# RMS norm and matrix product on one core: sixteen early words of output, smaller loads and last stores, and a last store issued outside the ordered section

## Chip, cores and metric

The kernel runs on one core of a Trainium2 chip. The metric is the device time of one execution in microseconds (us); the median of several executions counts, and less is better. The profile comes from one further look at a single execution with the hardware profiler on.

## What is computed

Each row of x (16 x 1024 rows of 512 numbers, float32) is divided by the root of its mean square, multiplied by gamma, and multiplied by a weight matrix of 512 x 768. The output is float32, 16 x 1024 x 768.

```
rms = np.sqrt(np.mean(x ** 2, axis=-1, keepdims=True) + eps)
x_norm = x / rms * gamma
return np.matmul(x_norm, weight).astype(np.float32)
```

So 33.6 MB of x and 1.6 MB of weights come in, and 50.3 MB of output go out.

## The kernel before

**Tiles.** The 16,384 rows are 128 tiles of 128 rows (NT). x is loaded in groups of 16 tiles (XG) into two buffers, xt0 and xt1; in a group each of the 128 partitions holds 16 rows that follow each other in memory. The output is collected in groups of 8 tiles (OG) in three buffers, ot0 to ot2, and stored from there. What one load or one store covers is set at lines 136 and 137 by `stretches`: a dictionary that gives, for some groups, the sizes into which the group is cut; a group without an entry is one transfer. In x, group 0 is cut into 2, 2, 4 and 8 tiles, groups 1, 2, 5, 6 and 7 into 8 and 8, and groups 3 and 4 (tiles 48 to 79) are whole. In the output, group 0 is cut into 2, 2 and 4, group 1 and the last one into 4 and 4, and all others are whole. A store of 8 tiles is 3 MB, a load of 16 tiles 4 MB.

**Work on a tile.** ScalarE squares the rows and sums them (`square`, L194), and takes the root of several tiles' sums at once (`root`, L199); VectorE inverts it (L201). GpSimd turns x into bf16 (`cast`, L186, and `cast_quad`, L258). Then x has to be transposed: for most tiles TensorE does it (L228) and VectorE copies the result out of PSUM (`evac`, L237); for the last four tiles of each later group VectorE transposes blocks of 32 x 32 (`move`, L269). The products run on TensorE: for each of four blocks of 128 features the transposed x is held (L294) and two products with the weights follow (L298), 512 and 256 wide. The finished tile is scaled on its way from PSUM to the output buffer by ScalarE (even tiles, L277) or VectorE (odd tiles, L279). The weights have been multiplied by gamma at the start by the same two lines.

**Order.** Nothing is issued while the program is described. `run` and `transfer` append each operation with the cells that it reads and writes to a list in the class `Order`. At the end `emit` walks through the list once. It keeps, for each engine, what that engine already knows to be done (`known`, a clock for each other engine and for each transfer), and finds the few waits that are needed (`needs`). Then it goes through the list again, puts the waits on the engines and issues the operations in the order of the list; each engine's queue holds its own in that order. A transfer gets a semaphore from a small set that is used again once some engine's knowledge shows that the earlier transfer on it has landed.

All of this stands in a critical section (L432). `emit` returns the marks of those transfers that no operation waited for, and a second section makes the SyncE queue (SP) wait for them (L435):

```
    with tc.tile_critical():
        left = order.emit()

    with tc.tile_critical():
        for sem, count in left:
            SP.wait_ge(sem, count)
```

**Queues.** All loads of x (L175), both weight loads (L343) and all stores (L291) are issued by SP, in one queue, in the order of the list: the first two tiles of x, the two weight loads, the rest of the first two x groups, and from there on stores as their tiles are finished, with the loads of a later x group between them. A store waits on SP for the last tile of its stretch; whatever is behind it on SP waits too. gamma alone is loaded by ScalarE's queue (L338). L468 is the line that the profile gives for what frames the kernel: branches, waits and the closing barrier of all engines.

Of the kernel before, what the change touches and what calls it, by code (L numbers as in the profile page):

```python
# [11 lines left out]
F32 = mybir.dt.float32  # L12
# [4 lines left out]
P = 128  # L17
# [3 lines left out]
class Order:  # L21
# [17 lines left out]
    def emit(self):  # L39
        nc = self.tc.nc  # L40
        streams = {id(e): n for n, e in enumerate((nc.tensor, nc.vector, nc.scalar, nc.gpsimd, nc.sync))}
        writer, readers = {}, {}
        known = [dict() for _ in streams]
        clocks, needs, place, slot_of, slots = [], [], [], {}, []
        count = [0] * len(streams)
        for n, (proc, engine, _, reads, writes) in enumerate(self.ops):
            at = streams[id(engine)]
            if proc is None:
                me, turn = ("transfer", n), 1
            else:  # L50
                count[at] += 1
                me, turn = at, count[at]
            written = {writer[cell] for cell in reads + writes if cell in writer}
            read = {d for cell in writes for d in readers.get(cell, ())}
            need = []
            for d in sorted(written | read, reverse=True):
                who, when = place[d]
                if who == me and (engine is nc.tensor or d not in written):
                    continue
                if known[at].get(who, 0) < when:  # L60
                    need.append(d)
                    for k, v in clocks[d].items():
                        known[at][k] = max(known[at].get(k, 0), v)
            if proc is None:
                free = [k for k, d in enumerate(slots) if known[at].get(("transfer", d), 0)]
                if free:
                    slots[free[0]] = n
                else:
                    slots.append(n)
                slot_of[n] = ("slot", slots.index(n))  # L70
            clock = dict(known[at])
            clock[me] = turn
            place.append((me, turn))
            clocks.append(clock)
            needs.append(need)
            for cell in reads:
                readers.setdefault(cell, []).append(n)
            for cell in writes:
                writer[cell], readers[cell] = n, []
        awaited = {d for need in needs for d in need}  # L80
        last = [n for n, (me, _) in enumerate(place) if not isinstance(me, int) and n not in awaited]
        sems, marks, done = {}, {}, {}
        for n in range(len(self.ops)):
            me = slot_of.get(n, place[n][0])
            if n in slot_of or n in awaited:
                if me not in sems:
                    sems[me] = self.tc.alloc_semaphore(f"done{len(sems)}")
                done[me] = done.get(me, 0) + (16 if n in slot_of else 1)
                marks[n] = (sems[me], done[me])
        for n, (proc, engine, issue, _, _) in enumerate(self.ops):  # L90
            for d in needs[n]:
                engine.wait_ge(*marks[d])  # L92
            ins = issue()
            if n in marks:
                ins.then_inc(marks[n][0], 16 if n in slot_of else 1)
        return [marks[n] for n in last]


@with_exitstack
def kernel(  # L100
# [8 lines left out]
    nc = tc.nc  # L109
    PE, DVE, ACT, POOL, SP = nc.tensor, nc.vector, nc.scalar, nc.gpsimd, nc.sync  # L110
    order = Order(tc)
# [5 lines left out]
    out = out.flatten_outer_dims()  # L117
    N, D = x.shape
    _, O = out.shape
    K = D // P  # L120
    NT = N // P
    NP = NT // 2
    XG, OG = 16, 8
    AHEAD = 20

    def stretches(group, parts):
        first, size, i = {}, {}, 0
        for g in range(NT // group):
            for n in parts.get(g, [group]):
                for t in range(i, i + n):  # L130
                    first[t], size[t] = i, n
                i += n
        return first, size

    last = NT // OG - 1
    x_first, x_size = stretches(XG, {0: [2, 2, 4, 8], **{g: [8, 8] for g in (1, 2, 5, 6, 7)}})
    o_first, o_size = stretches(OG, {0: [2, 2, 4], 1: [4, 4], last: [4, 4]})

    def rows(ap, i, n):
        base, t = (x_first[i], x_size[i]) if i < XG else (i - i % XG, XG)  # L140
        return ap[base * P:(base + t) * P, :].rearrange("(p t) d -> p t d", t=t)[:, i - base:i - base + n, :]

    def sb(name, shape, dtype):
        return nc.alloc_sbuf_tensor(name, shape, dtype).ap()
# [14 lines left out]
    ot = [sb(f"ot{n}", [P, OG, O], F32) for n in range(3)]  # L159
# [7 lines left out]
    def cells(name, slot, i, n=1):  # L167
        return [(name, slot, t) for t in range(i, i + n)]
# [4 lines left out]
    def load(i):  # L173
        dst, to = x_of(i, x_size[i])
        order.transfer(SP, lambda: SP.dma_start(out=dst, in_=rows(x, i, x_size[i])), writes=to)  # L175
# [3 lines left out]
    def load_until(i):  # L179
        while starts and starts[0] < i:  # L180
            load(starts.pop(0))
# [104 lines left out]
    def store(i):  # L286
        first, n = o_first[i], o_size[i]
        s = first // OG % 3
        if i == first + n - 1:
            src = ot[s][:, first % OG:first % OG + n, :]  # L290
            order.transfer(SP, lambda: SP.dma_start(out=rows(out, first, n), in_=src), reads=cells("ot", s, first % OG, n))  # L291

    def hold(lhsT, cell):
        run(PE, lambda: PE.ldweights(lhsT), [cell])  # L294
# [20 lines left out]
    def finish_tile(i, a, engine):  # L315
        s = i // OG % 3

        before = [("ot", s, i % OG - 1)] if i == o_first[i] + o_size[i] - 1 else []
        scale(engine, ot[s][:, i % OG, :], ops[a][:, :O], rstd[:, i:i + 1],
              [("ops", a, 0), ("ops", a, 1), ("rstd", i)] + before, [("ot", s, i % OG)])  # L320
        store(i)
# [20 lines left out]
    def load_weights(h):  # L342
        order.transfer(SP, lambda: SP.dma_start(out=w_f32[:, 2 * h:2 * h + 2, :].rearrange("p c o -> p (c o)"), in_=wv[:, h, :]),  # L343
                       writes=[("w_f", 2 * h), ("w_f", 2 * h + 1)])

    load_until(2)
    load_weights(0)
    load_weights(1)
    load_until(2 * XG)
# [79 lines left out]
            matmuls(i, a, range(K), feed)  # L429
            finish_tile(i, a, engine)  # L430

    with tc.tile_critical():  # L432
        left = order.emit()

    with tc.tile_critical():  # L435
        for sem, count in left:
            SP.wait_ge(sem, count)


# [33 lines left out]
```

## Time and profile before

| what | value |
|---|---|
| median of 7 executions | 209.79 us (209.57 to 210.37) |
| the profiled execution's own time | 209.57 us |
| its span, first to last instruction | 207.6 us |
| mean granted TensorE clock | 0.985 |
| HBM read, written | 35.13 MB, 50.33 MB |
| stores: 8 tiles, 4 tiles, 2 tiles | 13, 5, 2 |
| loads of x: 16 tiles, 8 tiles, 4, 2 | 2, 11, 1, 2 |

The page gives busy time by engine, then the span in 40 slices of 5.2 us each, then the DMA queues, and then the chain of work that ended last, followed back from the last instruction. "q1" is the queue that SP feeds; its share is the time that its packets took, as a share of sixteen DMA engines over the span. A row of the windows view gives, for one stretch of time, the busy time and number of instructions of each engine, the granted clock, the mean busy share of the sixteen DMA engines, and GB/s; packets are counted where they start, so a short window's share can be above 1. The lines for one source line give the durations of its instructions and, for a transfer, the time from its issue to its landing, which is when the last of its sixteen completion marks has come. In the timeline, what stands in square brackets is the engine's idle time before the instruction and what ended it.

The time of an execution is longer than the span of its instructions; here by 1.9 us.

### The profile page before, as it was taken

How to read it: one execution, taken by the hardware profiler on the slowest of the kernel's cores; microseconds unless marked ns; L12 is line 12 of the kernel's file. 1: busy time of each engine (PE TensorE's matmuls, PEld its weight loads, DVE VectorE, ACT ScalarE, POOL GpSimd, SP SyncE). 2: the span in 40 equal slices, each digit the busy share in tenths (PEclk: the TensorE clock that was granted, in tenths of full speed). 3: DMA queues.
4: the chain of work that ended last, by engine and by line, in shares of the span. 5: the costliest groups of instructions: out<-in, count | busy, mean ns of one | idle time of the engine just before them, and what ended most of it. 6: DMA issues, size and time to landing. Idle time of an engine off the chain costs nothing.

```text
span 207.6 us, 2784 instructions
## 1 busy us (share of the span) xinstructions
PE 194.9 (94%) x1236; PEld 72.7 (35%) x717; DVE 149.4 (72%) x255; ACT 144.4 (70%) x343; POOL 59.9 (29%) x34
## 2 busy tenths in 40 slices
PE   7889999999999999999999999999999999999910
PEld 1234434433344334332344334333343333343300
DVE  0455647998589957998579975999579975999410
ACT  4698897877768596855887687777787687763300
POOL 2247642046300390005800670007600363000000
PEclk9999999999999999999999999999999999999995
DMA  6999999999999999999999999999999999996994
GB/s 228 418 447 423 376 389 430 429 442 420 445 437 436 409 434 450 423 417 425 434 426 426 421 434 429 423 425 431 443 423 428 415 448 434 421 436 260 440 421 199
DMA packets 5488, 85.62 MB, mean 412 GB/s; under 512 B 610, under 2 KB 612, under 8 KB 1380
## 3 DMA queue, kind: packets, MB, share of 16 engines
q1 hardware_dynamic: 5472, 85.46, 97.2%
q8 instruction: 7, 0.11, 0.2%
q14 instruction: 5, 0.04, 0.0%
q10 hardware_dynamic: 4, 0.00, 0.0%
HBM read 35.13 MB, written 50.33 MB: 412 GB/s over the span
## 4 chain that ended last, share of the span: by engine, by line
PE 71%; DMA 16%; DVE 5%; issue 1%; SPq 1%; ACT 1%; POOL 1%; ACTq 0%
PE ps L298 63%; DMA xt<-in_x_dram 16%; PE ps L228 8%; DVE ot L279 2%; DVE xTq L269 2%; DVE xT L237 1%; POOL xb L186 1%; ACT jk L194 0%; SPq L343 0%; SPq L175 0%; ACT ot L277 0%; SPq L291 0%; DVE rstd L201 0%; SPq L468 0%; ACTq L92 0%
## 5 line engine op out<-in xcount | busy, mean ns | idle before, releaser
L298 PE MATMUL ps<-w_bf,xT 128*128 128x512 bf16 (+1 forms) x800 | 147.7, 326 | 0.8 <-ACT ot L277 0.4
L277 ACT ACTIVATE ot<-ps,rstd 128x768 f32<-128x768 f32 x64 | 57.5, 898 | 42.9 <-PE ps L298 41.3
L194 ACT ACTIVATE jk<-xt 128x512 bf16<-128x512 f32 x128 | 78.7, 618 | 6.8 <-DMA xt<-in_x_dram 6.8
L186 POOL CAST xb<-xt 128x2048 bf16<-128x2048 f32 (+3 forms) x21 | 46.4, 2221 | 112.4 <-DMA xt<-in_x_dram 112.4
L279 DVE TENSOR_SCALAR ot<-ps,rstd 128x768 f32<-128x768 f32 x64 | 64.8, 1013 | 9.0 <-PE ps L298 8.4
L294 PEld LDWEIGHTS <-xT 128*128 128x128 bf16 x400 | 39.3, 98 | 59.9 <-issue 52.0
L228 PE MATMUL ps<-ident_f,xb 128*128 128x128 f32 x200 | 54.4, 277 | 0.9 <-POOL xb L186 0.9
L237 DVE COPY xT<-ps 128x1024 bf16<-128x1024 bf16 (+1 forms) x53 | 34.5, 654 | 24.5 <-PE ps L228 22.9
L269 DVE STREAM_TRANSPOSE xTq<-xq 32x256 f32<-32x256 f32 x112 | 48.7, 435 | 3.4
L228 PEld LDWEIGHTS ps<-ident_f,xb 128*128 128x128 f32 x200 | 28.3, 143 | 46.4 <-issue 42.9
L298 PE MATMUL ps<-w_bf,xTq 128*128 128x512 bf16 x224 | 42.8, 326 | 0.0
L194 ACT ACTIVATION_READ_ACCUMULATOR jk<-xt 128x1 f32 x128 | 24.3, 190 | 0.0
L294 PEld LDWEIGHTS <-xTq 128*128 128x128 bf16 x112 | 11.0, 98 | 14.5 <-issue 14.5
L258 POOL CAST xq<-xt 128x2048 bf16<-128x2048 f32 x7 | 13.3, 1896 | 0.0
L201 DVE RECIPROCAL rstd<-rms 128x8 f32<-128x8 f32 (+3 forms) x20 | 3.9, 193 | 7.8 <-ACT rms L199 7.6
L199 ACT ACTIVATE rms<-ssq,eps_sb 128x8 f32<-128x8 f32 (+3 forms) x20 | 6.0, 300 | 0.6
L298 PE MATMUL ps<-warm 128*128 128x512 bf16 x10 | 4.8, 629 | 1.4 <-DVE eps_sb L352 1.4
L277 ACT ACTIVATE w_bf<-w_f,g_sb 128x768 bf16<-128x768 f32 x2 | 1.9, 936 | 1.3 <-DMA w_f<-in_weight_dram 1.3
L375 DVE COPY g_sb<-ps 128x4 f32<-128x4 f32 x1 | 0.2, 162 | 3.2 <-PE ps L369 3.2
L339 ACT ACT_TABLE_LOAD x1 | 1.3, 1283 | 1.5 <-SPq L432 1.5
L279 DVE TENSOR_SCALAR w_bf<-w_f,g_sb 128x512 bf16<-128x512 f32 (+2 forms) x3 | 1.4, 483 | 0.8 <-DMA w_f<-in_weight_dram 0.8
L369 PEld LDWEIGHTS ps<-ident_f,g_row 2*128 2x128 f32 x2 | 0.3, 202 | 2.6 <-issue 2.6
(10 smaller groups left out, 2.0 us busy)
## 6 DMA issues: line engine op xcount, KB each, us to landing
out_dram<-ot SPq DMA_DIRECT2D x13, 3072.0 KB, 15.8
xt<-in_x_dram SPq DMA_DIRECT2D x11, 2048.0 KB, 20.3
xt<-in_x_dram SPq DMA_DIRECT2D x2, 4096.0 KB, 22.8
out_dram<-ot SPq DMA_DIRECT2D x5, 1536.0 KB, 11.0
w_f<-in_weight_dram SPq DMA_DIRECT2D x2, 768.0 KB, 5.6
out_dram<-ot SPq DMA_DIRECT2D x2, 768.0 KB, 15.8
xt<-in_x_dram SPq DMA_DIRECT2D x2, 512.0 KB, 5.3
xt<-in_x_dram SPq DMA_DIRECT2D x1, 1024.0 KB, 9.2
```

Source lines behind the costliest of these rows:

```text
L186: run(POOL, lambda: POOL.tensor_copy(out=xb[s][:, i % 8:i % 8 + n, :], in_=src), of, cells("xb", s, i % 8, n))
L194: run(ACT, lambda: ACT.activation(out=jk[j], in_=src[:, 0, :], func=AF.Square, accum_out=ssq[:, i:i + 1]), of, [("jk", j), ("ssq", i)])
L199: run(ACT, lambda: ACT.activation(out=rms[:, s], in_=ssq[:, s], func=AF.Sqrt, scale=1.0 / D, bias=eps_sb), [("ssq", t) for t in range(i, i ...
L201: run(DVE, lambda: DVE.reciprocal(out=rstd[:, s], in_=rms[:, s]), [("rms", i)], [("rstd", t) for t in range(i, i + n)])
L228: run(PE, lambda: PE.transpose(out=tp[b][:, t, h, :], in_=words[:, lo:lo + P], identity=ident_f), cells("xb", s, j % 4 * 2 + t) + ["ident" ...
L237: run(DVE, lambda: DVE.tensor_copy(out=dst[:, t:t + n, :], in_=src[:, t:t + n, :]), [("tp", b)], cells("xT", j % 4, t, n))
L258: run(POOL, lambda: POOL.tensor_copy(out=xq[s], in_=src), of, [("xq", s)])
L269: run(DVE, lambda: DVE.transpose(out=dst, in_=src), [("xq", s)], [("xTq", s)])
L277: run(ACT, lambda: ACT.mul(out=dst, in_=src, mul=r), reads, writes)
L279: run(DVE, lambda: DVE.tensor_single_scalar(out=dst, in_=src, scalar=r, op=mybir.AluOpType.mult), reads, writes)
L294: run(PE, lambda: PE.ldweights(lhsT), [cell])
L298: run(PE, lambda: PE.add_instruction(mybir.InstMatmult(name=nc.get_next_instruction_name(), engine=mybir.EngineType.PE, ins=[PE.lower_ap(r ...
```

## The change

There are four edits.

1. *Sixteen words.* Behind the load of the first two tiles of x and ahead of the weight loads, SP issues a transfer of sixteen zeros from a constant to the output: the first word of every eighth row of the first 128 rows. Both this and the first store of output are listed as writing a cell "marks", so that the first store, which overwrites these words, waits for them.
2. *x in eights.* Every group of x from tile 16 on is loaded in two transfers of 8 tiles.
3. *Finer last stores.* The last group but one of the output is stored in 4 and 4 tiles, the last one in 4, 2 and 2.
4. *The last store.* `emit` issues all operations but the last in the list, which is the last store, and hands that one back. It is issued by SP behind the section, with a no-op of SP ahead of it; the framework itself then waits for its landing ahead of the closing barrier. The waits for the other stores that nobody has waited for are made by ScalarE's queue instead of SP's. Which these are is now asked of `known`: transfers of which no engine knows, directly or through others.

```diff
-        last = [n for n, (me, _) in enumerate(place) if not isinstance(me, int) and n not in awaited]
+        seen = {who for clock in known for who in clock}
+        last = [n for n, (me, _) in enumerate(place) if me not in seen and not isinstance(me, int)]
...
-        for n, (proc, engine, issue, _, _) in enumerate(self.ops):
+        for n, (proc, engine, issue, _, _) in enumerate(self.ops[:-1]):
...
-        return [marks[n] for n in last]
+        return [marks[n] for n in last if n < len(self.ops) - 1], self.ops[-1][2]
...
-    x_first, x_size = stretches(XG, {0: [2, 2, 4, 8], **{g: [8, 8] for g in (1, 2, 5, 6, 7)}})
-    o_first, o_size = stretches(OG, {0: [2, 2, 4], 1: [4, 4], last: [4, 4]})
+    x_first, x_size = stretches(XG, {0: [2, 2, 4, 8], **{g: [8, 8] for g in range(1, NT // XG)}})
+    o_first, o_size = stretches(OG, {0: [2, 2, 4], 1: [4, 4], last - 1: [4, 4], last: [4, 2, 2]})
...
-            order.transfer(SP, lambda: SP.dma_start(out=rows(out, first, n), in_=src), reads=cells("ot", s, first % OG, n))
+            order.transfer(SP, lambda: SP.dma_start(out=rows(out, first, n), in_=src), reads=cells("ot", s, first % OG, n),
+                           writes=["marks"] if first == 0 else [])
...
     load_until(2)
+
+    zeros = nc.const_aps.tensor(0.0, (16, 1), F32)
+    order.transfer(SP, lambda: SP.dma_start(out=out[:P, :1].rearrange("(e r) c -> e r c", r=8)[:, 0, :], in_=zeros,
+                                            allow_slow_non_contiguous=True), writes=["marks"])
     load_weights(0)
...
     with tc.tile_critical():
-        left = order.emit()
-
-    with tc.tile_critical():
+        left, last_store = order.emit()
+    with tc.tile_critical() as others:
         for sem, count in left:
-            SP.wait_ge(sem, count)
+            ACT.wait_ge(sem, count)
+    behind = SP.nop().ins
+    ordered = mybir.DependencyInfo(mybir.DependencyClass.NoSync, mybir.DependencyReason.SCHED_ONLY)
+    tc.add_manual_dep(behind, others.name, ordered)
+    ins = last_store().ins
+    tc.add_manual_dep(ins, behind.name, ordered)
+    tc.declare_no_dep(ins, others, reason="ScalarE only waits for the stores ahead of the last")
```

## The prediction

> **What bounds the kernel now.** I read the page first: engine totals, the slices, the DMA queues, the chain.
>
> ```profile
> PE 194.9 (94%) x1236; PEld 72.7 (35%) x717; DVE 149.4 (72%) x255; ACT 144.4 (70%) x343; POOL 59.9 (29%) x34
> DMA  6999999999999999999999999999999999996994
> GB/s 228 418 447 423 376 389 430 429 442 420 445 437 436 409 434 450 423 417 425 434 426 426 421 434 429 423 425 431 443 423 428 415 448 434 421 436 260 440 421 199
> q1 hardware_dynamic: 5472, 85.46, 97.2%
> ```
>
> TensorE is busy for 94% of the span, but the transfers are busy for 97.2% and run at some 426 GB/s from the second slice on, with one dip at 21 to 31 us (376, 389) and one at 187 to 192 (260). The chain doesn't settle which of the two sets the end: its last piece is DVE at L279, done at 199.1, 8.5 us before the span ends. The waits of the SP queue name what fills that hole, and the answer for line 291 gives issue and landing of single stores:
>
> ```profile
> SPq L468 <- DMA out_dram<-ot: 6.2, 1, 6.2
> L291 SPq DMA_DIRECT2D out_dram<-ot x1: 332/332/332, 199.2 to 199.2; - x1
> DMA to landing us min/median/max: 7.1/7.1/7.1
> L291 SPq DMA_DIRECT2D out_dram<-ot x1: 332/332/332, 176.9 to 176.9; - x1
> DMA to landing us min/median/max: 14.5/14.5/14.5
> ```
>
> The last store goes out at 199.15 and lands at 206.22. Its 1.57 MB at 426 GB/s are 3.7 us; the rest is queue. The store issued at 176.9 lands only at 191.4, although the next was in the queue from 189.4. The windows around it (busy time by engine, clock, DMA share, GB/s) show why:
>
> ```profile
> 2.50:187.00 184.50, 182.76 (x1167) 69.31 (x683) 140.97 (x242) 139.73 (x339) 59.23 (x28) 1.00 1.01 426
> 186.50:187.50 1.00, 1.00 (x8) 0.40 (x4) 0.93 (x3) 0.59 (x1) 0.00 (x0) 1.00 0.69 295
> 187.50:188.50 1.00, 1.00 (x9) 0.29 (x3) 0.94 (x3) 0.00 (x0) 0.00 (x0) 1.00 0.63 270
> 188.50:189.50 1.00, 1.00 (x9) 0.29 (x3) 0.97 (x2) 0.49 (x1) 0.00 (x0) 1.00 0.18 74
> 189.50:190.50 1.00, 1.00 (x9) 0.29 (x3) 0.93 (x3) 0.41 (x1) 0.00 (x0) 1.00 0.92 393
> ```
>
> The sixteen DMA engines are not level. From 188.5 to 189.5 a share of 0.18 is about three engines at work and thirteen idle. The trace's completion marks (sixteen to a transfer) agree: for that store they run from 187.42 to 191.40, the last three after 191.2. Those three never ran dry, and three are last again at the end (thirteen marks by 205.49, then 205.83, 205.86, 206.22). So **the slowest DMA engine, fed from 1.96 (first packet) to 206.22, sets the end**. A step counts if it shortens that engine's work or what follows its landing.
>
> **The change part by part.** The sum is made against this execution: span 207.63, its time 209.57, so 1.94 lie outside; the median shown, 209.79, is 0.22 above it.
>
> **Last store behind the section.** In the built program SP passes the section's end before it issues it: two waits on the other engines, a no-op, a branch. In the old program these stand behind the issue, at 199.53 to 199.95, some 0.07 each, and a branch took 0.12. So it issues about 0.35 later. The slowest engine hides that, since the store before it lands there at 202.57; with that cover gone it costs 0.35. On SP only the closing wait is queued behind. The gain is after the landing: SP wakes at 206.24, makes three more waits, a branch, a signal, a drain and a no-op, and reaches its first closing drain at 206.82. In the new program ACT makes those waits beside it, for stores that land a transfer earlier, and SP goes from the landing to that drain in one step (0.03). Worth -0.55.
>
> **Finer last stores.** Tiles 112 to 119 go in fours, 124 to 127 in twos: two transfers more. The half that is ready near 183.5 instead of 189.4 fills the hole at 187 to 190 for thirteen engines, and for the three last ones nothing. The trace's packet records: 24 KB take 912 ns (median), 12 KB 460, 6 KB 234, eight packets to an engine. Halving costs 8 x (2 x 460 - 912) = 0.06, and 8 x (2 x 234 - 460) = 0.06. Together +0.13.
>
> A rule speaks against this part and the next. The Trainium skill, "DMA: Bandwidth & Descriptors", section "Measured (HBM→SBUF, 128 partitions, SWDGE, issued from GpSimd)", says to batch transfers to 1 MiB or more: 341 GB/s there against 425 at 16 MB. By its time for 1 MB (6.15 us), against 2.5 us of pure data at 425, some 3.7 us would be lost with each further transfer, over 10 in all. The packet records above deny it for a full queue.
>
> **x in eights.** Only tiles 48 to 79 change, groups 3 and 4 (loads at 48.67 and 72.09, landing at 70.80 and 95.47). TensorE's one stall after the start goes:
>
> ```profile
> 95.56 0.63 ACT L194 ACTIVATE jk<-xt 128x512 bf16<-128x512 f32 x1 [2.73 <-DMA xt<-in_x_dram]
> 97.73 1.46 PE L298 MATMUL ps<-w_bf,xT 128*128 128x512 bf16 x8 [0.43 <-ACT ot L277]
> ```
>
> The first half comes some 5 us sooner (eight packets of 611 ns), which covers ACT's 2.73. But that is 0.43 us of an engine with slack: 0. The price is two transfers more, 8 x (2 x 611 - 1213) = 0.07 each: +0.14.
>
> The slack: last product 198.08, DVE 1.02, section 0.35, issue 0.33, 0.64 from issue to first packet (first load: 1.32 to 1.96), 8 x 0.234 = 1.87, 0.4 to the mark, 0.9 closing: 203.6 by way of TensorE, against a span of 207.63 now and 206.6 as summed below. About 3 us are free.
>
> **Sixteen words.** One more issue on SP, ahead of both weight loads and all other x loads, moves them by some 0.47 (issues at 0.94, 1.37, 1.84 now). Data moves from 1.96, and the first load marks its end at 3.81 to 4.29, so most is covered; TensorE's slack takes the rest. The packets themselves: the nearest rows are the 608 four-byte marks, 9 ns each. The first output store must now wait for it, but is issued only at 13.08. What it could bring stands in the first dip:
>
> ```profile
> 21.00:23.00 2.00, 2.00 (x15) 0.93 (x9) 0.95 (x3) 1.97 (x6) 1.08 (x1) 1.00 1.00 426
> 23.00:25.00 2.00, 2.00 (x15) 0.82 (x8) 1.01 (x2) 1.33 (x3) 2.00 (x1) 1.00 1.16 377
> 25.00:27.00 2.00, 2.00 (x15) 0.83 (x9) 1.62 (x2) 2.00 (x8) 0.52 (x1) 1.00 0.73 212
> 27.00:29.00 2.00, 2.00 (x16) 0.79 (x9) 0.94 (x2) 2.00 (x7) 0.24 (x1) 1.00 1.00 414
> ```
>
> From 23 to 27 the mean is 294.5 instead of 426: 4 x (1 - 294.5/426) = 1.23 us, lost by all sixteen engines alike (packets of 611 ns take up to 1387), just ahead of the first packets that write the output, which start at 26.5. Later turns from loads to stores show nothing like it on all engines. I read it as the price of the first write to a new place, which no row proves. The early words may pay it at the start, and more cheaply: the first packets of x took 215 or 509 ns more than the 159 of their kind, on each engine once. Bounds: -1.23 (gone, nothing in its place) to +1.23 (it stays and is paid a second time). I take -1.23 + 0.4 = -0.8, with the price from the first packets of x, the nearest first touch.
>
> No run here shows what the same page states under "Specifications", that below 512 B the engine reads, modifies and writes; it gives no time for it.
>
> **Sum:** -0.55 + 0.13 + 0.14 - 0.8 = -1.08. Span 206.55; time 208.49 by this execution, 208.7 by the median.
>
> **The rivals.** *The engines level out.* If the lag of the slowest (4.0 us at 187) is not rebuilt, the filled hole counts for it too. The engines that lag collect instruction fetches (seven packets of 16 KB on queue 8, most of them 0.88 to 1.0 us on one engine) and slow load packets where others have turned to stores; later work at the same moments argues for the same lag, but the loads of groups 3 and 4, where some of it grows, are cut. With the lag halved: 208.7 - 2.0 = 206.7; all gone, TensorE's 203.6 + 2.16 = 205.8.
>
> *The dip has another cause and the words are free.* Then -0.55 + 0.27 remain: 209.5, within what can be told. For it: the slow packets begin at 23.87, 2.6 us ahead of the first write.
>
> *Slower: the words stall the loads and the dip stays.* Place: between the first x load and the weights, where all data stands behind the words. Price: a first-write stall as long as the dip, 1.23, on every engine: -0.28 + 1.23 = +0.95, 210.7. It decides from 0.7 us on (0.28 + 0.42). Against it: the word is small, and x's own first touch cost at most 0.51.
>
> *The late issue counts.* Only if the queue is empty at 199.5; then the sum loses 0.35 but the levelled case holds, so it is no case of its own.
>
> **How the numbers follow.** 0.2% is 0.42 us, about what a measurement of this kernel tells from none. My forecast, 208.7 (its own range 208.2 to 209.3, from a dip gone for nothing to one of which four fifths are paid again): 0.48. Levelled engines: 0.17. Dip unmoved: 0.21. Slower: 0.14. Faster than 209.37 are the first two and a little of the third: 0.66; the same 0.21; slower 0.13. The range reaches from 206.7 (a halved lag; half of that case is left out) to 210.2, which leaves out the greater part of the slower case.
>
> **What would show it.** Right: GB/s at 23 to 27 near 426; no hole at 187 to 190; ACT and TensorE without the waits at 95.56 and 97.73; some 0.9 us from the last landing to the end of the span instead of 1.4; the last issue about 0.35 after DVE's end; last marks still spread by about 3 us. Wrong: the dip unmoved, or one as deep at 3 to 5 us with the first products late by a microsecond; the last marks within 1 us of each other (levelled); the last landing set by the last issue, which would make TensorE the bound.

## The result, and the profile after

The changed kernel takes 212.22 us in the median of 15 runs (210.47 to 213.61), the kernel before 209.86 (36 runs). The ratio is 1.0093, 95% interval [1.0074, 1.0112]: slower by 0.9%, where 0.5% faster was forecast. On a second chip, in five runs, it was 1.0095 [1.0053, 1.0138]. A ratio is worked out from the single runs, without those that took over 1.5% longer than the fastest of their kernel (here one of 214.67 us), so it can differ by some tenths of a percent from the quotient of the two medians (here 1.0112).

The first profile after is of that execution of 214.67 us, so a second profile of the same kernel is read here (run after_again; own time 211.03, span 208.9). Its page, in the lines that answer to those shown of before:

```profile
PE 195.9 (94%) x1236; PEld 72.8 (35%) x717; DVE 149.6 (72%) x255; ACT 144.8 (69%) x343; POOL 60.0 (29%) x34
DMA  4999999999999999999999999999999999999993
GB/s 153 355 444 430 430 385 435 431 430 414 430 369 430 367 445 428 417 424 439 436 430 424 436 427 431 422 438 439 424 433 409 442 441 417 442 433 409 426 419 162
q1 hardware_dynamic: 6080, 85.46, 97.3%
```

The bytes are the same and the hole at slice 36 (counted from 0) is gone. The dip at slices 4 and 5 has shrunk, but the first two slices carry 153 and 355 GB/s instead of 228 and 418, and there are new dips at slices 11 and 13 (369, 367). The windows put them side by side, first the kernel before, then the changed one (the last three columns are clock, DMA share and GB/s):

```profile
2.00:9.00 7.00, 6.72 (x25) 1.78 (x13) 2.26 (x7) 4.07 (x8) 1.17 (x2) 1.00 0.99 394
11.00:13.00 2.00, 1.82 (x12) 0.54 (x5) 1.75 (x4) 1.98 (x5) 0.95 (x1) 1.00 1.13 483
23.00:28.00 5.00, 5.00 (x35) 2.04 (x20) 2.62 (x4) 4.33 (x12) 2.52 (x1) 1.00 0.96 319
57.00:62.00 5.00, 5.00 (x35) 2.03 (x20) 4.24 (x7) 3.60 (x10) 0.00 (x0) 1.00 0.98 421
66.00:74.00 8.00, 8.00 (x53) 2.78 (x29) 7.64 (x14) 5.61 (x14) 3.08 (x1) 1.00 0.97 412
```

```profile
2.00:9.00 7.00, 4.99 (x16) 1.24 (x9) 0.98 (x4) 2.39 (x6) 1.16 (x2) 1.00 0.84 290
7.00:9.00 2.00, 0.00 (x0) 0.00 (x0) 0.00 (x0) 0.00 (x0) 0.00 (x0) 1.00 0.91 345
11.00:13.00 2.00, 2.00 (x8) 0.44 (x3) 0.62 (x1) 1.65 (x4) 0.69 (x1) 0.50 1.07 455
23.00:28.00 5.00, 5.00 (x36) 2.15 (x22) 2.63 (x5) 4.29 (x12) 3.77 (x2) 1.00 0.97 388
57.00:62.00 5.00, 5.00 (x36) 1.97 (x20) 3.32 (x5) 3.31 (x9) 0.00 (x0) 1.00 0.97 365
66.00:74.00 8.00, 8.00 (x54) 3.09 (x31) 7.64 (x14) 5.84 (x16) 3.60 (x1) 1.00 1.01 389
```

From 2 to 9 us GB/s fall from 394 to 290, and from 7 to 9 no compute engine runs at all. From 11 to 13 us TensorE's clock is 0.50 (before: 1.00). The lost time of the DMA engines can be put in microseconds: spread each packet's bytes over its duration, and compare what was moved in a stretch with a full rate of 430 GB/s. The sixteen engines together lost this much: from 2 to 9 us 2.38 instead of 0.72, 23 to 28 0.32 instead of 1.08, 44 to 52 0.31 instead of 0.12, 57 to 62 0.58 instead of 0, 66 to 74 0.80 instead of 0.03; up to 186 us 4.64 instead of 2.18. So most of the dip at 23 to 28 us, which the forecast hoped to remove, did go, but with what came elsewhere the loss grew by 2.5 us net.

The waits name what was late at the start. In the kernel before, ScalarE and VectorE wait little for the weights, and TensorE has no row of waiting for the scaled weights; in the changed kernel all three wait:

```profile
ACT w_bf L277 <- DMA w_f<-in_weight_dram: 1.3, 2, 1.1
DVE w_bf L279 <- DMA w_f<-in_weight_dram: 0.8, 1, 0.8
```

```profile
ACT w_bf L278 <- DMA w_f<-in_weight_dram: 4.0, 2, 3.1
DVE w_bf L280 <- DMA w_f<-in_weight_dram: 3.3, 2, 2.2
PE ps L300 <- DVE w_bf L280: 2.7, 1, 2.7
```

The first weight load lands at 9.15 us instead of 6.19, although it was issued only 0.49 later. The answers for the load's line, before (L343: the first of the two loads alone, then both) and after (L345, the first alone):

```profile
L343 SPq DMA_DIRECT2D w_f<-in_weight_dram x1: 420/420/420, 1.4 to 1.4; - x1
DMA to landing us min/median/max: 4.8/4.8/4.8
L343 SPq DMA_DIRECT2D w_f<-in_weight_dram x2: 420/422/424, 1.4 to 1.8; - x2
DMA to landing us min/median/max: 4.8/5.6/6.4
```

```profile
L345 SPq DMA_DIRECT2D w_f<-in_weight_dram x1: 409/409/409, 1.9 to 1.9; - x1
DMA to landing us min/median/max: 7.3/7.3/7.3
```

The first product moves from 7.28 to 9.72, and TensorE's end from 198.07 to 200.23. At the other end of the span, the windows around the old hole and after the last issue:

```profile
186.00:188.00 2.00, 2.00 (x15) 0.82 (x8) 1.94 (x5) 0.74 (x1) 0.00 (x0) 1.00 0.97 418
188.00:190.00 2.00, 2.00 (x15) 0.80 (x8) 1.87 (x5) 0.90 (x1) 0.00 (x0) 1.00 1.00 430
...
204.00:206.00 2.00, 0.00 (x0) 0.00 (x0) 0.00 (x0) 0.00 (x0) 0.00 (x0) 0.64 0.72 301
206.00:208.00 2.00, 0.00 (x0) 0.00 (x0) 0.00 (x0) 0.00 (x0) 0.00 (x0) 0.50 0.16 65
```

The hole is filled (0.97, 1.00). After 204 the engines finish one by one: the last store's marks run from 204.82 to 208.00. Its issue was done at 201.91; adding the forecast's terms (0.64 to the first packet, 1.87 of data, 0.4 to the mark) gives 204.82. So the path by way of TensorE is over with the first mark, and the slowest DMA engine sets the end, 3.2 us later. From the last landing to the end it is 0.91 instead of 1.41.

### The profile page after: what moved, and what is told of

Read it like the earlier page. It is cut to its first block, busy times and chain, and to the rows that moved or that the text cites. A ratio compares the mean times of both kernels' runs of the same rounds, so it can differ in the third digit from the quotient of the medians.

```text
span 212.6 us, 2798 instructions
## 1 busy us (share of the span) xinstructions
PE 195.4 (92%) x1236; PEld 72.7 (34%) x717; DVE 149.6 (70%) x255; ACT 144.2 (68%) x343; POOL 60.0 (28%) x34
## 4 chain that ended last, share of the span: by engine, by line
PE 71%; DMA 15%; DVE 5%; issue 1%; ACT 1%; SPq 1%; ACTq 0%
PE ps L300 63%; DMA xt<-in_x_dram 11%; PE ps L229 9%; DMA w_f<-in_weight_dram 4%; DVE ot L280 2%; DVE xTq L270 2%; DVE xT L238 1%; ACT jk L195 0%; ACT ot L278 0%; DVE w_bf L280 0%; SPq L351 0%; SPq L345 0%; SPq L176 0%; SPq L292 0%; DVE rstd L202 0%
## 5 line engine op out<-in xcount | busy, mean ns | idle before, releaser
L300 PE MATMUL ps<-w_bf,xT 128*128 128x512 bf16 (+1 forms) x800 | 149.2, 328 | 4.5 <-DVE w_bf L280 3.3
L300 PE MATMUL ps<-warm 128*128 128x512 bf16 x10 | 3.9, 530 | 1.4 <-DVE eps_sb L358 1.4
```

Source lines behind the costliest of these rows:

```text
L300: run(PE, lambda: PE.add_instruction(mybir.InstMatmult(name=nc.get_next_instruction_name(), engine=mybir.EngineType.PE, ins=[PE.lower_ap(r ...
```

## The experiments

Theory W: the sixteen words hold DMA engines up between 2 and 9 us (called the stop below), and this makes the whole loss. Rivals: the further transfers (S), or the late issue and new close (B). Ratios are against runs of the kernel before on the same chip. "Weights at" gives the landing of the first weight load in the run's profile; "..." stands for lines left out.

**One edit at a time.** The first run adds only the words:

```diff
...
     load_until(2)
...
+    order.transfer(SP, lambda: SP.dma_start(out=out[:P, :1].rearrange("(e r) c -> e r c", r=8)[:, 0, :], in_=zeros,
+                                            allow_slow_non_contiguous=True), writes=["marks"])
     load_weights(0)
```

> The kernel before with the sixteen words alone. Theory W (the words stop some DMA engines for 2 to 3 us at the start, as the profile after shows at 3.7 to 7 us, and these engines stay last): 211.5 to 213, with w_f landing near 9 us instead of 6.2. Rival S (the loss comes from the four further transfers, that is x in eights and finer stores): 209.5 to 210.1. Rival B (the loss comes from the late issue and the new close): 209.5 to 210.1. The forecast's own reading, that the words take away the dip at 23 to 27 us: 208.6 to 209.2.

Measured 211.93 us against 209.83, ratio 1.0114 [1.0083, 1.0145]; weights at 9.06. The second takes these lines, and the cell "marks", out of the changed kernel:

> The changed kernel without the sixteen words. Theory W: 209.0 to 209.6, a little below the kernel before, by the shorter close (0.55) less the price of further transfers (0.27). Rivals S and B: 211.5 to 212.5, as the changed kernel.

209.63 against 209.83, 0.9994 [0.9981, 1.0006]; weights at 6.31. The words make the whole loss, and S and B fall as its cause. The other three edits, each alone, follow. First the stores:

```diff
-    o_first, o_size = stretches(OG, {0: [2, 2, 4], 1: [4, 4], last: [4, 4]})
+    o_first, o_size = stretches(OG, {0: [2, 2, 4], 1: [4, 4], last - 1: [4, 4], last: [4, 2, 2]})
```

> The kernel before with the finer last stores alone. Theory W, with a slowest DMA engine that gains nothing from the filled hole at 187 to 190 us: 209.8 to 210.1 (+0.13). If the engines level out through it: 207 to 209. Rival S: 210.5 or more.

210.16 against 209.83, 1.0015 [1.0003, 1.0027]: a small loss, just above the expected 209.8 to 210.1. Its slowest engine lands at 206.44 (before 206.22) though the first is done at 202.76 (before 205.33): filling the hole brought nothing to the slowest. Then the last store behind the section (all lines of the change's fourth edit, at the top and the end of the diff in "The change"):

> The kernel before with the last store behind the section, and the other waits on ScalarE, alone. Theory W and the step of the forecast: 209.2 to 209.4 (0.55 less behind the landing, the late issue hidden by the queue). Rival B: 210.2 or more (the issue 0.35 late and nothing gained).

209.32 against 209.83, 0.9988 [0.9968, 1.0008]. The close is 0.90 us from the last landing, the last issue comes 0.30 after DVE's end (before 0.03). The interval holds 1, so the half microsecond is seen in the profile and the median and not settled in the ratio. Then x in eights:

```diff
-    x_first, x_size = stretches(XG, {0: [2, 2, 4, 8], **{g: [8, 8] for g in (1, 2, 5, 6, 7)}})
+    x_first, x_size = stretches(XG, {0: [2, 2, 4, 8], **{g: [8, 8] for g in range(1, NT // XG)}})
```

> The kernel before with x in eights from tile 16 alone. The forecast's step: ScalarE's 2.73 us and TensorE's 0.43 us of waiting at 95 to 98 us go, the time rises by 0 to 0.2: 209.8 to 210.1. Rival (the stall at 97.7 us is on the path to the end): 209.3 to 209.5. Rival (further transfers in mid-stream stop the queue as the sixteen words do): 210.5 or more.

210.03 against 209.94, 1.0008 [0.9997, 1.0020]. The two waits at 95 and 97 us are gone from the timeline, and TensorE ends 0.66 earlier (197.41), for nothing.

**What about the words does it?** First their place: behind all loads that are issued at the start.

```diff
     load_until(2 * XG)
...
+    order.transfer(SP, lambda: SP.dma_start(out=out[:P, :1]...), writes=["marks"])
```

> The kernel before with the sixteen words put behind all loads that are issued at the start, instead of between the first two. Theory P (the price is that weights and x stand behind a stopped queue, TensorE starts late by about 2.5 us and its stores with it): weights land near 6.2 us again, 209.6 to 210.2. Rival Q (a write of sixteen words does harm at any place, through the further dips that the run with the words alone shows at 44 to 74 us): 211 or more.

213.04, 1.0148 [1.0091, 1.0205]. The weights land at 6.19, so the start is whole, but this place has a price of its own: the first store may not overwrite the words before they have landed, which is at 28.07, and goes out at 28.15 instead of 13.08, with all stores and loads behind it. So the slower time says nothing for or against Q (harm at any place).

Next, sixteen pieces of 1 KB instead of 4 bytes, from a tile of zeros, whose filling is moved ahead of the loads in the list:

```diff
...
+    order.transfer(SP, lambda: SP.dma_start(out=out[:P, :256].rearrange("(e r) c -> e r c", r=8)[:, 0, :],
+                                            in_=warm[:16, :].bitcast(F32)), reads=["warm"], writes=["marks"])
```

> The kernel before with sixteen rows of 1 KB of zeros at the place of the sixteen words. If the first write to the output is what stops the engines: as the words alone, 211.5 to 212.5, weights at about 9 us. If writes as small as 4 bytes are the cause: 209.7 to 210.3, weights at about 6.3 us.

211.76, 1.0054 [1.0017, 1.0091] (209.67 to 214.14); weights at 8.60. The size of 4 bytes is not it. A read in place of the write:

```diff
...
+    order.transfer(SP, lambda: SP.dma_start(out=sixteen, in_=x[:P, :1].rearrange("(e r) c -> e r c", r=8)[:, 0, :],
+                                            allow_slow_non_contiguous=True), writes=["sixteen"])
```

> The kernel before with sixteen words read from x into a scratch tile (not used) at the place of the sixteen words. If a write to the output is the cause: 209.7 to 210.2, weights at about 6.3 us. If any transfer of sixteen small pieces there stops the queue: 211 to 212.5.

212.49, 1.0105 [1.0042, 1.0167]; weights at 8.66. So the stop is no matter of writing at all. Here are its windows:

```profile
2.00:9.00 7.00, 4.74 (x16) 1.40 (x9) 1.29 (x5) 2.66 (x7) 1.17 (x2) 1.00 0.88 294
23.00:28.00 5.00, 4.95 (x35) 2.13 (x22) 2.94 (x6) 4.29 (x11) 3.60 (x1) 1.00 0.97 396
```

The dip at 23 to 28 us is all but gone (396) though nothing had been written to the output by then, and none comes with the first writes (0.08 us lost from 28 to 44): it was not the price of a first write. The words at the other end of the output (`out[N - P:, :1]`, with the last store waiting for them):

> The kernel before with the sixteen words in the last 128 rows of the output instead of the first (the last store waits for them). If the price is that of the first write to the output as a whole: as the words alone, 211.5 to 212.5, and the dip at 23 to 27 us small. If it belongs to the place that is written: the stop at 3 to 7 us stays and the dip at 23 to 27 us is as in the kernel before, 211.5 to 213.5.

212.25, 1.0091 [1.0055, 1.0127]; weights at 9.17. Then 128 words, eight to an engine:

```diff
...
+    order.transfer(SP, lambda: SP.dma_start(out=out[:P, :1], in_=zeros, allow_slow_non_contiguous=True), writes=["marks"])
```

> The kernel before with 128 words (one from each partition, eight pieces to a DMA engine, as every other transfer has) at the place of the sixteen. If the count of pieces matters (one to an engine where all other transfers have eight): 209.8 to 210.4, weights at about 6.3 us. If the size of the pieces matters, or any further transfer at this place: 211.5 to 213.

212.12, 1.0106 [1.0055, 1.0157]; weights at 8.86. The count of pieces is not it. No small transfer at all, but the first load of x in two:

```diff
-    load_until(2)
+    for t in starts[:1] + [1]:
+        order.transfer(SP, lambda t=t: SP.dma_start(out=x_of(t)[0], in_=rows(x, t, 1)), writes=x_of(t)[1])
+    starts.pop(0)
```

> The kernel before with the first load of x (two tiles) cut into two loads of one tile: one further transfer at the same place, with the same bytes in all and pieces of 2 KB. If any further transfer there stops the queue: 211 to 213, weights at about 8.5 us. If only the sixteen-piece transfer does: 209.7 to 210.3, weights at about 6.3 us.

211.46, 1.0068 [1.0035, 1.0102]; weights at 8.47. So the stop needs neither small pieces nor the output: every further transfer tried there on SP's queue brings it. The words on ScalarE's queue (`ACT.dma_start`):

> The kernel before with the sixteen words issued by ScalarE's queue, behind gamma, instead of SP's. If the stop is in SP's ring, behind the short transfer: 209.7 to 210.3, weights at about 6.2 us. If the access itself stops the engines, whatever queue it comes from: 211 to 213.

209.93, 1.0004 [0.9991, 1.0016]; weights at 6.39. Here the words are written early (landed at 5.40), nothing stops, and the dip stays (0.94 us lost from 23 to 28 by the measure above, before 1.08): an early write does not take it away.

**The queue's length, the place, or the time?** Theory N counts the transfers that stand in SP's queue at once. One less at the start, without and with the words:

```diff
-    load_until(2 * XG)
+    load_until(XG + 8)
```

> The kernel before with seven transfers issued by SP at the start instead of eight: the load of tiles 24 to 31 goes behind the first store. Theory N (the dip at 23 to 27 us, which falls on the eighth transfer, comes from the number that stand in SP's queue at once): the dip goes, 208.6 to 209.3. If the dip belongs to the first turn from loads to stores, wherever it stands: it moves with the first store to about 22 us and the time is 209.6 to 210.3.

210.54, 1.0038 [1.0015, 1.0061]. The dip moved from 23 to 28 us to the last transfer ahead of the first store, before 23 (GB/s from 9 to 23: 387, before 434); by N it should have gone.

> The kernel before with the sixteen words, and the load of tiles 24 to 31 behind the first store: eight transfers at the start, as in the kernel before. Theory N: weights land near 6.3 us, 209.6 to 210.3. If what counts is that a transfer stands ahead of the weights: weights near 9 us and 211.4 to 212.6, as with the words alone.

212.09, 1.0081 [1.0043, 1.0118]; weights at 9.43. N falls. The same shorter start in the changed kernel without the words:

> The changed kernel without the words and with the load of tiles 24 to 31 behind the first store. Theory N: 208.4 to 209.1, below both kernels (the dip gone, the close shorter, stores finer). If the dip only moves: 209.4 to 209.9.

209.89, 0.9993 [0.9975, 1.0011]: no better than no_words with the longer start. Then the words behind the weights:

```diff
     load_weights(1)
...
+    order.transfer(SP, lambda: SP.dma_start(out=out[:P, :1]...), writes=["marks"])
     load_until(2 * XG)
```

> The kernel before with the sixteen words behind the two weight loads instead of ahead of them. If what counts is that the weights are issued late: weights near 6.2 us, no stop, 209.6 to 210.3. Theory N, and any rule by which a further transfer in SP's queue stops what is behind it: a stop at 7 to 12 us in the loads of x, 210.8 or more.

210.02, 1.0001 [0.9986, 1.0016]. The answer for the weight load, and the windows:

```profile
L344 SPq DMA_DIRECT2D w_f<-in_weight_dram x1: 420/420/420, 1.4 to 1.4; - x1
DMA to landing us min/median/max: 4.6/4.6/4.6
```

```profile
2.00:9.00 7.00, 6.64 (x27) 1.97 (x14) 2.34 (x7) 4.28 (x8) 1.17 (x2) 1.00 1.02 410
23.00:28.00 5.00, 5.00 (x34) 1.93 (x19) 2.57 (x5) 4.54 (x11) 2.16 (x1) 1.00 0.96 281
```

The same nine transfers, the same words, landed at 8.1 us: no stop at the start, and the dip at 23 to 28 deeper than before (281, before 319). The last test has no further transfer. SP only holds the first weight load back until a small GpSimd operation is done; for this, GpSimd's two operations on `ident_f` stand earlier in the list, but they start when they did:

```diff
...
+    run(POOL, lambda: POOL.memset(late, 0.0), [], ["late"])
...
         order.transfer(SP, lambda: SP.dma_start(out=w_f32[:, 2 * h:2 * h + 2, :].rearrange("p c o -> p (c o)"), in_=wv[:, h, :]),
+                       reads=["late"] if h == 0 else [],
                        writes=[("w_f", 2 * h), ("w_f", 2 * h + 1)])
```

> The kernel before with no further transfer, but with the first weight load held back on SP until a small GpSimd operation ends at about 1.8 us, so that it is issued when it is issued behind the sixteen words (1.86). If the time of issue of the weights is what counts (first x data moves from 1.96): weights near 8.5 to 9 us, 211 to 212.5. If a further transfer in the queue ahead of them is needed: weights near 6.3 us, 209.7 to 210.3.

211.02, 1.0042 [1.0013, 1.0070], single runs from 209.33 to 212.15. In the profile:

```profile
L343 SPq DMA_DIRECT2D w_f<-in_weight_dram x1: 333/333/333, 1.7 to 1.7; - x1
DMA to landing us min/median/max: 8.0/8.0/8.0
```

```profile
2.00:9.00 7.00, 4.31 (x16) 0.97 (x9) 0.98 (x4) 2.39 (x6) 1.17 (x2) 1.00 0.93 310
23.00:28.00 5.00, 5.00 (x36) 2.18 (x22) 2.55 (x6) 4.29 (x12) 3.76 (x2) 1.00 1.00 410
```

Issued at 1.75 instead of 1.37, the weights land at 9.75. What the words do is here without them: the stop, and the faded dip. So no further transfer is needed; what all profiles with the stop share is a first weight load issued at 1.75 or later. That is the cause as far as these runs show it. Two limits belong to it. The profiled execution is the slowest of the ten (212.15), and the median of this run lost 1.2 us where the words alone lost 2.1. The fastest single runs lie where the kernel before lies, so 1.75 may be near the edge; which of the other nine had the stop is not known. And a late issue is not slow by itself: in the kernel before, the second weight load is issued at 1.84 and lands at 8.23, 2.04 us behind the first. It is the first load of the weights that must not be late; whether a load of x in its place would suffer as much was not tried.

Finally, the changed kernel again, the profile used above:

> The changed kernel once more, for a second profile of it. If the stop at 3 to 9 us is the rule and not an accident of the first profile: about 1.3 us more lost there than in the kernel before, first products late by 2 to 2.6 us, 211 to 213. The marks of the last store spread by 1 to 5 us, where a slowest engine sets the end, or within 1 us, where TensorE's late stores do.

211.09 on that chip, as expected; the marks spread by 3.2 us, so the slowest engine sets its end.

## Why the prediction was wrong

*The step that failed* is the one on the sixteen words, in both halves. The first half said that the delay of the later loads by 0.47 us was mostly covered, because the first x load moves until about 3.8 to 4.3, and that TensorE's slack takes the rest. The delay itself was right (0.49). But over all profiles the weights' landing has two values: issued at 1.37 or 1.38, the first of the two loads lands at 5.98 to 6.46 (ten kernels); issued at 1.75 to 1.86, at 8.47 to 9.75 (the changed kernel and eight others). First data moves at 1.96. In the ten late profiles (two are of the changed kernel) the longest packet of the weights takes 1.01 to 2.28 us, in the ten early ones at most 0.63. So 0.4 to 0.5 us on a queue that looked covered moved the landing by 2.0 to 3.8.

The other half read the dip at 23 to 27 us as the price of a first write, which the early words would pay: -0.8 net. words_read (no early write, no dip) and words_act and words_mid (an early write, dip in place) refute it. In seven_first the dip moves to the load that is then the last ahead of the first store. In most profiles with the stop it fades, and others come at 44 to 74 us; but words_1kb keeps 0.89 us of it, and words_seven 1.26 at 9 to 23 us. What makes it stays open. That GB/s at 23 to 28 us rose from 319 to 388 looks like the forecast's first sign of being right; it came with the stop and not through the write, so it is luck and does not support the forecast.

*Measured sizes.* Predicted for the words -0.8, measured +2.1 (211.93 against 209.83). For the rest -0.28, measured -0.2 without the words (no_words, with an interval that holds 1). By parts: the close -0.55, in the profile 1.41 to 0.91, so -0.50; the late issue 0.35 and hidden, 0.29 and hidden; finer stores +0.13, some +0.3; eights +0.14, some +0.1 with an interval that holds 1. The bound by the slowest DMA engine held, too: the hole was filled for thirteen engines without gain, and TensorE's 0.43 us were worth nothing. Two readings of the forecast were off without bearing on this. The first packets of the output start at 26.70, not 26.5. And the estimate of 3.7 us for a further transfer rests on a row of the Trainium skill, "DMA: Bandwidth & Descriptors", section "Measured (HBM→SBUF, 128 partitions, SWDGE, issued from GpSimd)", whose time and rate do not fit each other: 1 MB in 6.15 us is 170 GB/s, not 341. Here four further transfers cost some 0.4 us in all (0.33 for the two stores, 0.09 for the two loads), near the 0.27 from the packet rows.

*TensorE's slack* of 3 us was worked out for the finer stores and held there (first mark 204.82, last 208.00). In words_only, with coarse stores, it does not: all sixteen marks come within 0.16 us of each other (207.89 to 208.05), behind a store of 8 tiles that was issued at 191.95 instead of 189.40. TensorE ends 2.55 us later than before (200.62) and the first mark comes 2.56 later: there the late start sets the end, not a slow engine.

*The rivals.* The slower one (words stall the loads, 210.7) had the right place. Its price was too low (1.23, where the stretch from 2 to 9 us alone lost 1.66 more), its cause was another, the dip did not stay, and it did not see that later dips, at 44 to 74 us, would add 1.5. "The dip has another cause" was right as to the cause. I priced the delay by cover, that is by whether the queue would run dry, and never asked whether the same load, issued against engines already at work, takes as long.

## What to carry to other kernels

Before something is put ahead of a load that the first products wait for, compare issue and landing of that load, not the queue's cover: half a microsecond on SP was 3 us on landing here. A transfer that must be early could go behind those loads (210.0) or on another queue (209.9) here, at no cost that could be measured. And where the transfers are at 97%, look at the sixteen completion marks: a hole that only the quicker engines have was worth nothing here.

## What the runs showed that was not expected

The stop itself: in words_only, single 6 KB packets of the weights took up to 1.9 us instead of 0.234, and some engines stood idle for 1.4 to 1.6 us between x and weights (packet records). Why a first weight load that comes 0.4 us later is taken so badly, and why dips then come at 44 to 74 us, no run shows.

TensorE's clock followed. In the changed kernel TensorE stands still for 2.73 us, from 6.99 to 9.72, and the trace's clock records then have 0.50 from 9.99 to 13.40; the kernel before has 1.00 there. Nine of the ten profiles with late weights have one such stage of 3.41 us near the start; first_split, with a pause of 2.67 us, has none, and neither have the ten others. The Trainium skill, "TensorE: Matmul & The Clock Gate", section "Part 1: The HAM clock gate (the "warmup" mystery)", says that the clock is halved after at least one idle window of about 3.4 us. The stage has that length, but the pause ahead of it is shorter: the 3.41 us before 9.99 begin at 6.58, when TensorE was still at work. A pause of 2.73 us was enough here, one of 2.29 in words_128 too, and one of 2.67 in first_split was not; so its length alone does not decide.

No kernel tried is faster than the kernel before by more than its interval leaves open; without the words the change is level with it (0.9994).
